# Row sums of a 16384 x 1024 matrix: one of nine loads is summed by one instruction over twelve rows in place of eight paired sums

## The chip, the core and the metric

The kernel runs on one core of a Trainium2 chip. The metric is the device time of one execution in microseconds (us), the median of several runs. The core has VectorE (DVE in the profile), ScalarE (ACT), GpSimd (POOL), TensorE (PE, not used here) and SyncE (SP), each with an instruction queue of its own, and 16 DMA engines that move data between the device memory and the core's SBUF. The only order among the queues is what semaphores enforce. A DMA is issued on a queue (here SP's and, for two stores, ACT's) and lands later; instructions that need its data wait for the landing.

## What is computed

The input has 32 x 512 rows of 1024 float32 values. Every row is summed.

```python
def setup_inputs():
    batch, seq, dim = 32, 512, 1024
    return {"x": np.random.randn(batch, seq, dim).astype(np.float32)}

def reference(x):
    return np.sum(x, axis=-1).astype(np.float32)
```

The input is 67.1 MB, the output 64 KB.

## The kernel before

The 16384 rows are spread over the 128 partitions, 128 rows to a partition, in three blocks: a head of 7 rows per partition (`HEAD`), seven loads of 15 rows each (`BIG`, `LOADS`), and a last block of 16 rows (`LAST`). "A row" below always means one row on each of the 128 partitions, that is 128 x 1024 values. One partition's rows of a block lie side by side in memory, and a load brings n rows to each partition in one DMA. All sums go to one tile, `sums`, with a column for each of the 128 rows (`[P, J]`).

The input tiles `t` come from a pool with three buffers (`bufs=3`, L140), taken in turn: the head has the first, the seven loads the second, third, first, second, third, first and second, and the last block the third. The loads are issued on SP's queue in the order of the program. A load into a buffer waits until the tile that had it before has been read; so the loads of the last block wait for the reduction of the fifth big load.

`rows()` (L182) does one load and sums its rows. It takes the number of rows that ScalarE sums (`n_act`) and whether VectorE sums in pairs. The rest of the rows are VectorE's:

- without `pairs`, one `tensor_reduce` (L148, TENSOR_REDUCE in the profile) reads all of VectorE's rows and writes a sum for each;
- with `pairs`, each row is a `tensor_tensor_reduce` of its own (`halves`, L162; CUSTOM_DVE_ANT_0 in the profile). It adds the second half of the row to the first, writes the 512 results in place, and accumulates their total. Reading the accumulator is a second short instruction (DVE_READ_ACCUMULATOR2_ANT).
- ScalarE's rows are an activation with function Copy each (`act`, L175, ACTIVATE), with a running total that is read out by ACTIVATION_READ_ACCUMULATOR. The copied values go to a PSUM tile, `unread`, that nobody reads (four buffers).

Head and first six big loads use `tensor_reduce` alone, with no ScalarE rows (`rows(t, 0, x_h, 0, 0)` and the `if` in the loop over `g`, L203 to L207). The seventh big load (`g == 6`, L209) gives 7 rows to ScalarE and 8 to VectorE in pairs.

The last block comes in pieces, each a DMA of its own: 7 rows (3 of them ScalarE's), 6 rows (2), 2 rows (1), and the last row in two parts of 536 and 488 values (L224, L225). The last row is summed by two `halves` one after the other: the first leaves its total in the column ahead of the second part, and the second then adds that column with the rest (L228, L229; L222 zeroes the column behind). Three stores write the result: the head's sums early (L200, on ACT's queue), the sums of the seven big loads (L226, `early`, on ACT's queue behind ScalarE's last row, held until the two-row piece has landed), and the last 16 sums (L230, on SP's queue), which end the program.

The order of work on each engine is the order of the program (`manual_schedule`). Three small functions rearrange instructions when the program is finished (first load at the entry, order of the waits of one instruction, a wait at the end); the change doesn't touch them.

Of the kernel before, what the change touches and what calls it, by code (L numbers as in the profile page):

```python
# [101 lines left out]
def kernel(  # L102
# [12 lines left out]
    rows = batch * seq  # L115
    J = rows // P
    HEAD, BIG, LOADS = 7, 15, 7
# [21 lines left out]
    with (  # L139
        tc.tile_pool(name="in", bufs=3) as inpool,  # L140
        tc.tile_pool(name="unread", bufs=4, space=bass.MemoryType.PSUM) as upool,
        tc.tile_pool(name="stage", bufs=1) as stpool,
        tc.manual_schedule(),
    ):
        sums = stpool.tile([P, J], fp32)

        def vec(dst, src):
            return nc.vector.tensor_reduce(  # L148
                out=dst, in_=src, axis=mybir.AxisListType.X, op=mybir.AluOpType.add
            )  # L150

        def hold(inst, until, reason):
            tc.add_manual_dep(
                inst.ins,
                until.ins.name,
                mybir.DependencyInfo(mybir.DependencyClass.Sync, mybir.DependencyReason.DATA),
                reason=reason,
            )

        def halves(dst, src):  # L160
            n = src.shape[-1] // 2
            return nc.vector.tensor_tensor_reduce(  # L162
                out=src[:, :n],
                in0=src[:, :n],
                in1=src[:, n:],
                scale=1.0,
                scalar=0.0,
                op0=mybir.AluOpType.add,
                op1=mybir.AluOpType.add,
                accum_out=dst,  # L170
            )

        def act(dst, src, n):
            unread = upool.tile([P, dim], fp32)
            nc.scalar.activation(  # L175
                out=unread[:, :n],
                in_=src,
                func=mybir.ActivationFunctionType.Copy,
                accum_out=dst,
            )  # L180

        def rows(t, a, src, j, n_act, pairs=False):  # L182
            n = src.shape[1]
            nv = n - n_act
            part = t[:, a * dim : (a + n) * dim].rearrange("p (n d) -> p n d", d=dim)
            load = nc.sync.dma_start(out=part, in_=src)  # L186
            if pairs:
                for q in range(nv):
                    done = halves(sums[:, j + q : j + q + 1], part[:, q, :])
            else:  # L190
                done = vec(sums[:, j : j + nv], part[:, :nv, :])
            for q in range(nv, n):
                act(sums[:, j + q : j + q + 1], part[:, q, :], dim)
            return load, done


        size = LAST * dim + 4
        t = inpool.tile([P, size], fp32)
        rows(t, 0, x_h, 0, 0)
        nc.scalar.dma_start(out=out_h, in_=sums[:, :HEAD])  # L200


        for g in range(LOADS):  # L203
            t = inpool.tile([P, size], fp32)
            src = x_m[:, g * BIG : (g + 1) * BIG, :]
            if g < LOADS - 1:
                rows(t, 0, src, HEAD + g * BIG, 0)  # L207
            else:
                rows(t, 0, src, HEAD + g * BIG, 7, pairs=True)  # L209


        j = HEAD + RUN
        t = inpool.tile([P, size], fp32)
        rows(t, 0, x_l[:, :7, :], j, 3, pairs=True)
        rows(t, 7, x_l[:, 7:13, :], j + 7, 2, pairs=True)
        two, _ = rows(t, 13, x_l[:, 13:15, :], j + 13, 1, pairs=True)


        c, width = pieces
        a = LAST - 1  # L220
        whole = t[:, a * dim + c : LAST * dim + 2]
        nc.vector.memset(whole[:, width + 1 :], 0.0)  # L222
        part = t[:, a * dim : a * dim + c]
        nc.sync.dma_start(out=part, in_=x_l[:, a, :c])  # L224
        nc.sync.dma_start(out=whole[:, 1 : width + 1], in_=x_l[:, a, c:])  # L225
        early = nc.scalar.dma_start(out=out_m, in_=sums[:, HEAD : HEAD + RUN])  # L226
        hold(early, two, "its packets come behind those of the loads")
        halves(whole[:, :1], part)  # L228
        halves(sums[:, J - 1 : J], whole)  # L229
        nc.sync.dma_start(out=out_l, in_=sums[:, j:])  # L230
# [30 lines left out]
```

## Time and profile before

| what | value |
|---|---|
| median of 3 runs | 162.27 us (162.22 to 162.77) |
| the profiled execution, whole | 162.26 us |
| its span in the profile | 160.1 us |
| VectorE busy | 116.1 us (73%) |
| ScalarE busy | 15.2 us (10%) |
| bytes read, mean rate over the span | 67.11 MB, 420 GB/s |

The span is the time from the first to the last instruction of the profiled execution; 2.2 us of its own time lie outside it. The profile names an instruction by line, engine, operation, what it writes and what it reads (`sums<-t`), with shapes as partitions x elements. "Idle before" is the time in which the engine had nothing to do ahead of an instruction, and the name behind the arrow is what ended it. A busy share is an average over stages that may have different limits, so the stage around the change has to be read for itself.

### The profile page before, as it was taken

The numbers are of one execution on the slowest core, as the hardware profiler recorded it, in microseconds if no ns is written. First come the engines' busy times: TensorE is split into PE (matmuls) and PEld (weight loads), VectorE is DVE, ScalarE is ACT, GpSimd is POOL, SyncE is SP. The second block draws the span as 40 slices with busy tenths as digits, with TensorE's granted clock in tenths as the row PEclk, the third lists the DMA queues.
The fourth block names the chain that finished last, engine by engine and source line by source line (L and its number), as shares of the span: only waits on it lengthen the run. The fifth ranks groups of instructions, "written<-read, shape, count | busy, mean of one in ns | idle before, by whom it ended". The sixth has DMA issues, their size and how long they took to land.

```text
span 160.1 us, 148 instructions
## 1 busy us (share of the span) xinstructions
DVE 116.1 (73%) x46; ACT 15.2 (10%) x27; POOL 0.2 (0%) x4
## 2 busy tenths in 40 slices
DVE  0029600699959998699959999599959999573345
ACT  0000210000000000000000000000000000496443
POOL 0000000000000000000000000000000000000000
DMA  8899997999699979998899969996999799899992
GB/s 301 387 475 491 491 415 323 492 492 445 292 491 491 461 307 461 491 491 368 368 491 491 445 292 491 491 461 276 491 491 461 307 461 491 344 451 410 418 390 98
DMA packets 2304, 67.18 MB, mean 420 GB/s; under 512 B 640, under 2 KB 768, under 8 KB 896
## 3 DMA queue, kind: packets, MB, share of 16 engines
q1 hardware_dynamic: 2016, 67.12, 97.6%
q10 hardware_dynamic: 288, 0.06, 0.2%
HBM read 67.11 MB, written 0.07 MB: 420 GB/s over the span
## 4 chain that ended last, share of the span: by engine, by line
DMA 76%; DVE 20%; SPq 1%; issue 0%; DVEq 0%
DMA t<-in_x_dram 76%; DVE sums L148 20%; SPq L186 1%; SPq L224 0%; DVE t L162 0%; DVEq L256 0%
## 5 line engine op out<-in xcount | busy, mean ns | idle before, releaser
L148 DVE TENSOR_REDUCE sums<-t 128x15 f32<-128x15360 f32 (+1 forms) x7 | 104.5, 14934 | 31.6 <-DMA t<-in_x_dram 31.6
L175 ACT ACTIVATE unread<-t 128x1024 f32<-128x1024 f32 x13 | 13.2, 1013 | 123.3 <-DMA t<-in_x_dram 123.3
L162 DVE CUSTOM_DVE_ANT_0 t<-t 128x512 f32<-128x512 f32 (+2 forms) x19 | 11.5, 661 | 10.6 <-DMA t<-in_x_dram 10.4
L175 ACT ACT_TABLE_LOAD x1 | 1.3, 1283 | 19.2 <-DVE sums L148 19.2
L175 ACT ACTIVATION_READ_ACCUMULATOR unread<-t 128x1 f32 x13 | 2.4, 186 | 0.0
L162 DVE DVE_READ_ACCUMULATOR2_ANT sums<- 128x1 f32 x18 | 1.5, 83 | 0.0
L245 POOL MEMSET const-bfloat16-1.0<- 128x1 bf16 x1 | 0.1, 102 | 0.0
L245 POOL MEMSET const-uint8-127<- 128x1 uint8 x1 | 0.1, 102 | 0.0
L245 POOL MEMSET const-float32-1.0<- 128x1 f32 x1 | 0.1, 99 | 0.0
L245 POOL MEMSET const-float32-0.0<- 128x1 f32 x1 | 0.1, 98 | 0.2 <-issue 0.2
L162 DVE DVE_READ_ACCUMULATOR2_ANT t<- 128x1 f32 x1 | 0.1, 83 | 0.0
L222 DVE MEMSET t<- 128x1 f32 x1 | 0.1, 59 | 0.0
## 6 DMA issues: line engine op xcount, KB each, us to landing
t<-in_x_dram SPq DMA_DIRECT2D x7, 7680.0 KB, 38.2
t<-in_x_dram SPq DMA_DIRECT2D x2, 3584.0 KB, 19.9
t<-in_x_dram SPq DMA_DIRECT2D x1, 3072.0 KB, 35.7
t<-in_x_dram SPq DMA_DIRECT2D x1, 1024.0 KB, 37.7
t<-in_x_dram SPq DMA_DIRECT2D x1, 268.0 KB, 37.9
t<-in_x_dram SPq DMA_DIRECT2D x1, 244.0 KB, 38.0
out_dram<-sums ACTq DMA_DIRECT2D x1, 52.5 KB, 1.7
out_dram<-sums ACTq DMA_DIRECT2D x1, 3.5 KB, 21.8
```

The lines of the kernel that those rows point to most:

```text
L148: return nc.vector.tensor_reduce(out=dst, in_=src, axis=mybir.AxisListType.X, op=mybir.AluOpType.add)
L162: return nc.vector.tensor_tensor_reduce(out=src[:, :n], in0=src[:, :n], in1=src[:, n:], scale=1.0, scalar=0.0, op0=mybir.AluOpType.add, op ...
L175: nc.scalar.activation(out=unread[:, :n], in_=src, func=mybir.ActivationFunctionType.Copy, accum_out=dst,)
L186: load = nc.sync.dma_start(out=part, in_=src)
L222: nc.vector.memset(whole[:, width + 1 :], 0.0)
L245: nc = _bacc.Bacc("TRN2", target_bir_lowering=False, num_devices=1)
```

## The change

In the seventh big load, ScalarE gets 3 rows in place of 7, and VectorE's 12 rows are one `tensor_reduce` in place of 8 paired sums.

```diff
             if g < LOADS - 1:
                 rows(t, 0, src, HEAD + g * BIG, 0)
             else:
-                rows(t, 0, src, HEAD + g * BIG, 7, pairs=True)
+                rows(t, 0, src, HEAD + g * BIG, 3)
```

The load itself, its place in SP's queue, and all that follows in the program are the same text.

## The prediction

> **What bounds the kernel now.** I read the chain of work that ended last first, because it says which resource an edit must touch to move the end; then the same chain in order of time, for its last part; then the groups kept apart by shape, for prices; then the timeline from 120 us on, where the changed load is summed.
>
> The page's chain:
>
> ```profile
> DMA t<-in_x_dram 76%; DVE sums L148 20%; SPq L186 1%; SPq L224 0%; DVE t L162 0%; DVEq L256 0%
> ```
>
> The chain in order of time (start us, us, what), its last pieces:
>
> ```profile
> 101.86 16.16 DVE sums L148
> 118.02 0.02 issue
> 118.04 0.33 SPq L186
> ...
> 119.42 0.43 SPq L224
> 119.85 0.04 issue
> 119.89 37.98 DMA t<-in_x_dram
> 157.87 0.02 issue
> 157.90 0.42 DVE t L162
> ```
>
> The 20% of VectorE in the chain are two reductions, and the later one is the fifth big load's (101.86 to 118.02): it frees the buffer for the last block, whose loads are then issued at once. From 119.89 to 157.87 the chain is nothing but those loads on their way. So the end is set by when the last bytes land, and every load has been issued before the changed rows are touched at 138.15. Only three things in the change could move the end: VectorE being late for the last row, ScalarE being late, or the transfers themselves becoming faster or slower.
>
> Prices, by shape (busy us, mean ns, idle before):
>
> ```profile
> L148 DVE TENSOR_REDUCE sums<-t 128x15 f32<-128x15360 f32 x6 | 96.9, 16153 | 20.5 <-DMA t<-in_x_dram 20.5
> L148 DVE TENSOR_REDUCE sums<-t 128x7 f32<-128x7168 f32 x1 | 7.6, 7620 | 11.1 <-DMA t<-in_x_dram 11.1
> ```
>
> And the timeline of the stage (start us, us, engine, instruction):
>
> ```profile
> 120.00 16.15 DVE L148 TENSOR_REDUCE sums<-t 128x15 f32<-128x15360 f32 x1 [1.99 <-DMA t<-in_x_dram]
> 138.15 1.03 ACT L175 ACTIVATE unread<-t 128x1024 f32<-128x1024 f32 x1 [117.67 <-DMA t<-in_x_dram]
> 138.16 0.69 DVE L162 CUSTOM_DVE_ANT_0 t<-t 128x512 f32<-128x512 f32 x1 [2.00 <-DMA t<-in_x_dram]
> ...
> 143.06 0.08 DVE L162 DVE_READ_ACCUMULATOR2_ANT sums<- 128x1 f32 x1
> ...
> 146.82 0.69 DVE L162 CUSTOM_DVE_ANT_0 t<-t 128x512 f32<-128x512 f32 x1 [3.68 <-DMA t<-in_x_dram]
> ...
> 149.28 0.08 DVE L162 DVE_READ_ACCUMULATOR2_ANT sums<- 128x1 f32 x1
> ...
> 154.13 0.69 DVE L162 CUSTOM_DVE_ANT_0 t<-t 128x512 f32<-128x512 f32 x1 [4.77 <-DMA t<-in_x_dram]
> ...
> 156.69 0.34 ACTq L226 DMA_DIRECT2D out_dram<-sums  x1
> 157.25 0.08 DVE L162 DVE_READ_ACCUMULATOR2_ANT sums<- 128x1 f32 x1
> 157.28 0.06 DVE L222 MEMSET t<- 128x1 f32 x1
> 157.30 0.44 DVE L162 CUSTOM_DVE_ANT_0 t<-t 128x268 f32<-128x268 f32 x1
> ```
>
> The reader is to see VectorE finish the seventh load at 143.14 (143.06 + 0.08), wait 3.68 us for the 7-row piece, finish that at 149.36 and wait 4.77 us for the 6-row piece. These two waits are the cover under which the change's extra work must fit.
>
> **VectorE's part.** Removed: eight pairs, 138.16 to 143.14, 4.98 us. Added: one reduction of 12 rows. The trace has 7 rows (7.620 us) and 15 rows (16.153 us); the slope is (16.153 - 7.620) / 8 = 1.0666 us a row, so 12 rows take 7.620 + 5 x 1.0666 = 12.95 us. The difference is 7.97 us more VectorE work. It begins when the load lands, as the pairs did, and ends at 138.16 + 12.95 = 151.11. The 7-row piece has by then been there since 146.82, so its four pairs follow directly: 149.36 - 146.82 = 2.54 us, to 153.65. The 6-row piece lands at 154.13. So 7.97 us go into 3.68 + 4.77 = 8.45 us of waiting, and 0.48 us are left: from 154.13 on VectorE runs as before. Price on the path: 0.
>
> If that cover were gone, VectorE would be late at 154.13 by some D. Two more small covers follow: the fifth pair of the last block could start at 156.58 and started with its landing at 156.63 (0.05 us), and the very last sum could start about 157.81, estimated from its predecessor's read at 157.66 plus its 0.08 and a hand-over of the same size, and started at 157.90 (about 0.09 us). So the end moves by D - 0.14, and by over 0.5% (0.81 us, about what a measurement of this kernel can tell from no change) only when VectorE comes 0.48 + 0.14 + 0.81 = 1.43 us later than worked out.
>
> Here the Trainium skill speaks against the change. Its page "VectorE: DVE Perf Modes", section "Rules for kernel authors", says of `tensor_reduce` on a hot path that it is the slowest VectorE operation and to restructure. The rows agree on the ratio (1.067 us a row against 4.98 / 8 = 0.62 us for a pair). With VectorE on the path, the sum would be 7.97 us more, 170.2 us; by the rows of waiting it is 0 and 162.3 us. I go by the rows, since the path is not hot for VectorE here.
>
> **What no row shows.** First, a pair straight behind a reduction: before, 2.00 us of waiting always stood between the last reduction (over at 136.15) and the first pair. The bounds are -0.08 us (pairs start 0.61 us apart though each takes 0.69) and 2.00 us (all that the wait could have hidden). The nearest row is the pair behind the MEMSET, which starts at 157.30, 0.02 us after the MEMSET's start and before its end, with a change of operation in between. I take 0. Second, a reduction while ScalarE also reads: all six long ones ran alone. The bounds are 0 and 2.3%, by which ScalarE's own first row beside a pair (1.03 us) is longer than later ones (1.005): 0.30 us on 12.95. Pairs took 0.69 us throughout beside ScalarE, so I take 0. Both at their upper ends would be 2.30 us.
>
> **ScalarE's part.** Four rows fewer, 1.04 us each from start to start (138.15, 139.21, 140.25). Its three rows end at about 141.4 in place of 145.54, and its next row waits for the landing at 146.82 either way. Cost and gain 0. The store of the big loads' sums (L226) needs all of them: the last is now ready at 151.11, not 145.54, but the store stands behind ScalarE's last row and was issued at 156.69, 5.6 us later. Cost 0 until the reduction ends 5.6 us late. Nothing is queued behind that store on ACT.
>
> **DMA and buffers.** No transfer is added, removed or moved. The second buffer, which holds the seventh load, is not taken again, so releasing it at 151.11 instead of 145.54 delays nobody. SP has issued everything by 120.4 us and then waits for the last sums. The transfers could still feel what the engines do to SBUF. Big loads landed 18.14 us apart (101.86 to 120.00, 120.00 to 138.15), with a reduction beside them nearly all the time; by their rate a 7-row piece takes 18.14 x 7/15 = 8.47 us. The one beside the eight pairs took 146.82 - 138.15 = 8.67 us, 0.20 us more. If pairs or ScalarE's rows are the cause, that much may come back; if reading by two engines at once is, it may grow with the stretch. The bounds are -0.20 us and, for 12.95 us in place of 4.98, 0.20 x 12.95 / 4.98 - 0.20 = +0.32 us. I take 0, as what caused the 0.20 isn't shown.
>
> **The sum** against the profiled execution: span 160.1 + 0 + 0 + 0, and its own time 162.26 us, stays. That execution lies 0.01 us from the median of 162.27, so the forecast is 162.25 us, rounded; its own range is 162.05 to 162.6 by the transfer bounds.
>
> **Rivals.**
>
> *VectorE comes late (slower).* The place is the hand-over from the 12-row reduction to the first pair of the 7-row piece. It costs something between 0 and 2.00 us that the wait before it hid. From 0.62 us on it moves the end, and from 1.43 us on by over 0.5%. At the full 2.00 us, the pairs end at 155.65, D = 1.52, and the end moves by 1.38 us: 163.65 us. For it: the margin is thin, 0.48 us of 8.45, and no row shows this pair of instructions. Against it: the MEMSET's row, and the straight-line price of a reduction, which six rows within 0.002 us of each other support.
>
> *The transfers gain.* The 0.20 us of the 7-row piece come back, and all later pieces land earlier by as much: 162.05 us. VectorE, ready at 153.65, is still ahead of a landing at 153.93. For it: the slow piece is the one beside the eight pairs. Against it: the 6-row piece, beside four pairs, took 7.31 us where the big loads' rate gives 7.26, so pairs alone don't explain it.
>
> *The transfers lose.* Reduction and ScalarE together slow them by up to 0.32 us: 162.6 us, inside 0.5%. Against it: six reductions beside transfers at the full 18.14.
>
> That the edit does less than it says has no footing: the loop's last turn takes the changed branch and no other.
>
> **Chances.** Forecast 0.54, transfers gain 0.14, transfers lose 0.12, VectorE late by enough to show 0.16, and 0.04 for a gain over 0.5% that no row speaks for. So faster 0.04, same 0.80, slower 0.16. The range runs from 161.9, just below the transfers' gain, to 163.1, 0.5% above the time before; the late VectorE at 163.65 and the unexplained gain are what it leaves out, 0.20 together.
>
> **What would show it.** Right: one L148 instruction 128x12 of 12.95 us from about 138.16; the first pair of the 7-row piece at 151.1 with no idle time before it; VectorE idle under 1 us ahead of the 6-row piece and still released by DMA; the last pieces of the chain as before. Wrong: a reduction over 13.4 us, a gap of over half a microsecond behind it, or the chain ending in VectorE rather than in DMA. Landings of the 7-row piece nearer than 8.67 us to the seventh load's would speak for the transfers' gain, and farther ones for their loss.

## The result, and the profile after

| | before | changed |
|---|---|---|
| median of 17 runs each | 162.34 us (162.22 to 162.82) | 161.93 us (161.69 to 162.24) |
| profiled execution, whole | 162.26 us | 161.99 us |
| its span | 160.08 us | 160.20 us |
| whole minus span | 2.18 us | 1.79 us |

The ratio is 0.9971, with a 95% interval of 0.9964 to 0.9979: 0.29% faster, small but clear of the scatter. The last two rows are the surprise: the profiled span has become longer by 0.12 us while the whole time has become shorter by 0.27. Over the 17 runs of the changed kernel the span's median is 160.1 us; over the runs of the kernel before that came with the experiments it is 160.1 to 160.2. Nothing that can be told from scatter was won inside the span.

The first lines of the page of the changed kernel, and its chain:

```profile
span 160.2 us, 123 instructions
...
DMA t<-in_x_dram 77%; DVE sums L148 20%; SPq L186 1%; SPq L224 0%; DVE t L162 0%; DVEq L256 0%
```

Its chain in order of time, the last pieces:

```profile
120.21 37.79 DMA t<-in_x_dram
158.00 0.02 issue
158.03 0.42 DVE t L162
```

Its timeline of the changed stage:

```profile
138.45 12.96 DVE L148 TENSOR_REDUCE sums<-t 128x12 f32<-128x12288 f32 x1 [1.99 <-DMA t<-in_x_dram]
...
146.95 1.03 ACT L175 ACTIVATE unread<-t 128x1024 f32<-128x1024 f32 x1 [5.27 <-DMA t<-in_x_dram]
...
151.32 0.68 DVE L162 CUSTOM_DVE_ANT_0 t<-t 128x512 f32<-128x512 f32 x1
...
154.27 0.69 DVE L162 CUSTOM_DVE_ANT_0 t<-t 128x512 f32<-128x512 f32 x1 [0.42 <-DMA t<-in_x_dram]
...
156.82 0.34 ACTq L226 DMA_DIRECT2D out_dram<-sums  x1
```

The reader is to see that the stage does what was worked out. The 12-row reduction takes 12.96 us; the first pair starts behind it at 151.32 with no idle time; of the 8.45 us in which VectorE waited before, 0.42 are left, ended by the landing of the 6-row piece; the chain is the last loads on their way, as before. The page counts 123 instructions, where the kernel before had 148. Of these, VectorE has 31 where it had 46, and this turned out to be the number that matters.

### The profile page after: what moved, and what is told of

The parts are those of the page before. It is cut to its first block, busy times and chain, and to the rows that moved or that the text cites. A ratio compares the mean times of both kernels' runs of the same rounds, so it can differ in the third digit from the quotient of the medians.

```text
span 160.2 us, 123 instructions
## 1 busy us (share of the span) xinstructions
DVE 124.0 (77%) x31; ACT 11.1 (7%) x19; POOL 0.2 (0%) x4
## 4 chain that ended last, share of the span: by engine, by line
DMA 77%; DVE 20%; SPq 1%; issue 0%; DVEq 0%
DMA t<-in_x_dram 77%; DVE sums L148 20%; SPq L186 1%; SPq L224 0%; DVE t L162 0%; DVEq L256 0%
## 5 line engine op out<-in xcount | busy, mean ns | idle before, releaser
L148 DVE TENSOR_REDUCE sums<-t 128x15 f32<-128x15360 f32 (+2 forms) x8 | 117.5, 14687 | 33.9 <-DMA t<-in_x_dram 33.9
L175 ACT ACTIVATE unread<-t 128x1024 f32<-128x1024 f32 x9 | 9.1, 1016 | 127.3 <-DMA t<-in_x_dram 127.3
L162 DVE CUSTOM_DVE_ANT_0 t<-t 128x512 f32<-128x512 f32 (+2 forms) x11 | 6.5, 641 | 0.6 <-DMA t<-in_x_dram 0.6
L175 ACT ACTIVATION_READ_ACCUMULATOR unread<-t 128x1 f32 x9 | 1.7, 187 | 0.0
L162 DVE DVE_READ_ACCUMULATOR2_ANT sums<- 128x1 f32 x10 | 0.8, 84 | 0.0
```

The costliest lines, as they stand in the source:

```text
L148: return nc.vector.tensor_reduce(out=dst, in_=src, axis=mybir.AxisListType.X, op=mybir.AluOpType.add)
L162: return nc.vector.tensor_tensor_reduce(out=src[:, :n], in0=src[:, :n], in1=src[:, n:], scale=1.0, scalar=0.0, op0=mybir.AluOpType.add, op ...
L175: nc.scalar.activation(out=unread[:, :n], in_=src, func=mybir.ActivationFunctionType.Copy, accum_out=dst,)
```

## The experiments

Two theories stood at the start. **Theory T** (transfers, a rival of the prediction): the 7-row piece lands 8.50 us behind the seventh load (138.45 to 146.95) in place of 8.67, so the pairs or ScalarE's rows had slowed it. **Theory I** (instructions): the time outside the span, whole minus span, depends on the program's instructions. It is a good measure, since each run has both numbers: in the 26 runs of the kernel before that came with the first four experiments, the whole time went from 162.04 to 162.81 us, but whole minus span stayed between 2.13 and 2.23.

Each edit below is against the changed kernel, if nothing else is said. "Outside" is the mean of whole minus span over a run's executions, with spans given to 0.1 us. "VectorE instructions" counts all that the record of the profiled execution has on VectorE's queue, waits and barriers included: 55 before and 39 after (the page counts only the work among them, 46 and 31). ScalarE's are 39 before and 30 after.

### One part of the change at a time, and instructions alone

First run: the seventh load by one reduction, over 8 rows, and 7 rows on ScalarE as in the kernel before.

```diff
-                rows(t, 0, src, HEAD + g * BIG, 3)
+                rows(t, 0, src, HEAD + g * BIG, 7)
```

> Seventh load: one reduction of 8 rows, ScalarE keeps 7 rows. Against before, only the eight pairs are gone (15 VectorE instructions fewer), ScalarE's part is as before. Theory I (instructions: the time outside the span, 2.18 us before and 1.79 us after, follows the number of instructions of the program): outside about 1.95 if all instructions count alike (15 of 25 gone), 1.79 if only VectorE's count; whole time 162.34 - 0.23 = 162.1 or 161.95. Theory T (transfers: the 7-row piece lands 8.67 us behind the seventh load before and 8.50 after, and the pairs are what slows it): piece at 8.50, outside 2.18, whole time about 162.15. If ScalarE's rows slow the piece: 8.67. The reduction should take 8.69 us and end about 0.03 us behind the landing of the piece, which costs nothing.

Second run: 3 rows on ScalarE as in the changed kernel, and VectorE's 12 rows in pairs.

```diff
-                rows(t, 0, src, HEAD + g * BIG, 3)
+                rows(t, 0, src, HEAD + g * BIG, 3, pairs=True)
```

> Seventh load: 12 rows in pairs (24 VectorE instructions), 3 rows on ScalarE (8 fewer than before). The program has as many instructions as before. Theory I with all alike: outside 2.18, whole time 162.34 (same as before); with VectorE's alone: above 2.18, about 2.4, whole time 162.5. Theory T with pairs as the cause: the 7-row piece lands 8.67 us or more behind the seventh load (pairs last 7.4 us in place of 5.0: up to 8.77), whole time 162.34 to 162.45; with ScalarE's rows as the cause: 8.50 to 8.55 and about 162.15.

Third run: the changed kernel with idle instructions on VectorE, in its first wait.

```diff
+        idle = stpool.tile([P, 16], fp32)
+        for q in range(16):
+            nc.vector.memset(idle[:, q : q + 1], 0.0)
         rows(t, 0, x_h, 0, 0)
```

> The changed kernel with 16 one-column MEMSETs on VectorE ahead of the first reduction, where VectorE waits 11 us. No work on the path changes. Theory I: outside goes back by 16/25 of 0.39 us to about 2.04 (all alike) or fully to 2.18 (VectorE's alone); whole time 162.15 to 162.35. Theory T: nothing changes, 161.93, with the piece at 8.50.

Fourth run: the changed kernel with idle instructions on ScalarE.

```diff
+        idle = stpool.tile([P, 16], fp32)
+        nc.vector.memset(idle[:, :8], 0.0)
+        for q in range(4):
+            act(idle[:, 8 + q : 9 + q], idle[:, :8], 8)
         rows(t, 0, x_h, 0, 0)
```

> The changed kernel with four 8-column activations, each with its accumulator read (8 ScalarE instructions, as many as the change removed there), and one MEMSET on VectorE, all in the first 11 us. Theory I, all alike: outside 1.79 + 9/25 of 0.39 = 1.93, whole time 162.07; if ScalarE's instructions alone count: 2.18 and 162.34; if VectorE's alone: 1.79 to 1.81 and 161.95. Theory T: 161.93.

| run | VectorE instr. | median us | ratio to before | outside us |
|---|---|---|---|---|
| reduction of 8, ScalarE 7 | 39 | 161.83 | 0.9969 [0.9956, 0.9981] | 1.79 |
| 12 pairs, ScalarE 3 | 63 | 162.16 | 0.9985 [0.9976, 0.9994] | 1.98 |
| changed + 16 MEMSETs | 55 | 162.34 | 1.0004 [0.9995, 1.0012] | 2.18 |
| changed + 4 activations | 40 | 161.89 | 0.9975 [0.9965, 0.9984] | 1.79 |

Sixteen MEMSETs that do nothing for the result, in a stretch where VectorE waits anyway, take the whole gain back. Eight extra instructions on ScalarE do nothing. The twelve pairs were expected above 2.18 us by the reading that more VectorE instructions cost more; they gave 1.98, with more instructions. So it isn't a price per instruction.

Theory T has no footing in these runs: the 7-row piece came 8.52 us behind the seventh load beside twelve pairs, and 8.59 beside the 8-row reduction. Runs below settle it.

### The shape: how outside time goes with VectorE's instructions

The same edit with other numbers of MEMSETs (4, 8, 12, 14, 20, 24, 32, 40) in the changed kernel.

> The changed kernel with 4 one-column MEMSETs ahead of the first reduction, as 16 of them in the run that gave 2.18 us outside the span (39 VectorE instructions in the profile without them, 55 with 16). Theory I-slope (each VectorE instruction adds 0.39/16 = 0.024 us outside the span): outside 1.89, whole time 162.0. Theory I-step (the outside time jumps where VectorE's program passes some length): outside 1.79 or 2.18 and nothing between.

> The same with 8 MEMSETs (47 VectorE instructions). Theory I-slope: outside 1.99. Theory I-step: 1.79 or 2.18.

> The same with 12 MEMSETs (51 VectorE instructions). Theory I-slope: outside 2.08. Theory I-step: 1.79 or 2.18, and 2.18 if 8 already gave it.

> The same with 24 MEMSETs, which makes 63 VectorE instructions, as many as the kernel with 12 pairs and 3 ScalarE rows, whose outside time was 1.97. If the number of VectorE instructions sets the outside time whatever their kind: 1.97 here too, below the 2.18 of 16 MEMSETs, so no slope and no single step. If the kind matters (MEMSETs of line 201 against pairs in the middle of the program): the slope gives 1.79 + 24 x 0.024 = 2.37, a single step 2.18.

> The changed kernel with 14 MEMSETs, 53 VectorE instructions. The outside time was 1.79 at 51 and 2.18 at 55. Theory boundary (a fetch of VectorE's program comes into the end once the program passes a boundary): 1.79 or 2.18, a jump between two neighbours. Theory of a gradual rise: about 1.98.

> The same with 20 MEMSETs, 59 VectorE instructions, between 55 (2.18) and 63 (1.96). Theory boundary, with the fetch triggered ever earlier as more of the program lies behind the boundary: between 2.18 and 1.96, about 2.07. If 63 is a plateau of its own: 2.18 or 1.96.

> The same with 40 MEMSETs, 79 VectorE instructions. Theory boundary, with the fetch ever earlier and at last hidden under the span: 1.79, and the instruction packet no longer behind the span's end. If the program beyond 63 costs as much as at 63: 1.96. If every instruction beyond adds time: above 2.2.

> The changed kernel with 32 MEMSETs, 71 VectorE instructions. From 55 to 63 the outside time fell by 0.027 us an instruction; at 71 that gives 1.75, so the floor of 1.79 or just above it, with the instruction packet at the end of the span or earlier. Theory moved cost: if the packet comes while loads still run, span 160.4 and whole time 162.2; if it comes behind the last load (157.6) and before the end, span 160.1 and 161.9. Theory hidden cost: 161.9 either way.

| VectorE instr. | kernel | outside us | span median us | whole median us | ratio to before |
|---|---|---|---|---|---|
| 39 | changed | 1.78 | 160.1 | 161.93 | 0.9971 [0.9964, 0.9979] |
| 43 | + 4 | 1.80 | 160.1 | 161.91 | 0.9978 [0.9966, 0.9990] |
| 47 | + 8 | 1.79 | 160.2 | 161.99 | 0.9985 [0.9973, 0.9996] |
| 51 | + 12 | 1.78 | 160.3 | 162.05 | 0.9975 [0.9962, 0.9987] |
| 53 | + 14 | 1.78 | 160.1 | 161.86 | 0.9968 [0.9955, 0.9981] |
| 55 | + 16 | 2.18 | 160.2 | 162.34 | 1.0004 [0.9995, 1.0012] |
| 59 | + 20 | 2.08 | 160.1 | 162.18 | 1.0001 [0.9989, 1.0014] |
| 63 | + 24 | 1.95 | 160.25 | 162.18 | 0.9994 [0.9983, 1.0005] |
| 71 | + 32 | 1.78 | 160.4 | 162.19 | 0.9994 [0.9985, 1.0003] |
| 79 | + 40 | 1.79 | 160.45 | 162.23 | 0.9992 [0.9981, 1.0004] |

A flat floor up to 53, a jump of 0.4 us within the next two instructions, then a fall of about 0.03 us an instruction to the floor again. The trace shows what falls. Each row below is a stretch of half a microsecond, with its length, the busy time of VectorE, ScalarE and GpSimd, the clock, the DMA engines' share and GB/s; behind it, in a fence of its own, the line of the DMA view for what lies after the span. With 20 MEMSETs:

```profile
161.40:161.90 0.50, 0.00 (x0) 0.00 (x0) 0.00 (x0) 1.00 0.00 0
161.90:162.40 0.50, 0.00 (x0) 0.00 (x0) 0.00 (x0) 1.00 0.05 16
```

```profile
q14 instruction: 1, 0.01, 1.0%
```

With 24:

```profile
161.40:161.90 0.50, 0.00 (x0) 0.00 (x0) 0.00 (x0) 1.00 0.05 16
161.90:162.40 0.50, 0.00 (x0) 0.00 (x0) 0.00 (x0) 1.00 0.00 0
```

One packet of instructions, 8192 bytes, starts 1.87 us behind the span's end with 59 VectorE instructions and 1.14 us behind it with 63. With 40 MEMSETs (79) it has moved into the span, to 143.49 us, between the packets of the loads. The DMA view from 143 to 144 us:

```profile
q1 hardware_dynamic: 15, 0.43, 103.9%
q14 instruction: 1, 0.01, 2.0%
```

With 71 it stands at 152.18 us. With 53 or fewer, no packet of instructions stands near the end or later than the first microsecond of the span. With 55, where the outside time is longest, none is in the record either; by the others it would start later still, and whether it comes too late to be recorded stays open.

So from some length of VectorE's program on, a packet of instructions is recorded late, and the more of the program there is, the earlier it comes. Whether it is one packet more in all can't be counted, as the records hold between 4 and 7 packets of this size ahead of the span, whatever the kernel. The record names no engine for it; it is taken for VectorE's because its time follows VectorE's count.

With the packet inside the span the gain does not come back. The span's medians with 71 and 79 are 160.4 us, 0.3 us above the changed kernel's; the outside time is back at its floor, and the whole time, at 162.2 us, is not. That the packet takes this time from the loads is shown only in part. It takes 0.31 us (79) and 0.33 us (71), and in the record one packet of the loads starts as it ends and takes 1.72 us where others of its size take 1.06 (with 71, 1.57 where others take 0.91). So it holds up one stream of the loads; whether that is the stream that the end waits for is another matter. The last loads in the chain with 71:

```profile
120.61 37.78 DMA t<-in_x_dram
```

With 79:

```profile
120.14 37.97 DMA t<-in_x_dram
```

The changed kernel has 37.79 and the kernel before 37.98, both with no such packet. In the profiled execution with 71 the packet therefore cost the end nothing; its span, 160.60 us, is long because the first load landed at 11.81 us, where the changed kernel's landed at 11.43. The idle MEMSETs themselves are a rival for the longer spans: 24 of them, with the packet behind the span, gave 160.25 us. What lengthens the spans at 71 and 79 stays open.

### The same in the kernel before, with the seventh load untouched

Fewer VectorE instructions (48), with the eight pairs and ScalarE's seven rows kept:

```diff
-        rows(t, 0, x_l[:, :7, :], j, 3, pairs=True)
+        rows(t, 0, x_l[:, :7, :], j, 3)
```

> The kernel before, with its eight pairs in the seventh load and ScalarE's 7 rows kept. Only the 4 VectorE rows of the 7-row piece are one reduction, which takes 4.42 us (7.620 - 3 x 1.0666) and ends at 151.24, before the landing at 154.13. VectorE has 48 instructions in place of 55. Theory length (the number of VectorE's instructions sets the time outside the span: 1.79 from 39 to 51, 2.18 at 55, 1.96 at 63): outside 1.79, whole time 161.95. Theory seventh load (what the change does to the seventh load's rows is the cause): nothing changes, 162.3.

More (63 and 79), as the MEMSETs above with 8 and 24 in the kernel before:

> The kernel before with 8 one-column MEMSETs ahead of the first reduction, 63 VectorE instructions. Theory length: outside 1.96, so more instructions and a shorter time, 162.1, and an instruction packet of 8 KB a good microsecond behind the span's end, as in the kernel of 12 pairs. Theory seventh load, and any theory by which instructions cost time each: 162.3 or more.

> The kernel before with 24 one-column MEMSETs, 79 VectorE instructions. With 79 in the changed kernel the outside time was back at 1.79 and an instruction packet of 0.31 us stood at 143.5, inside the span, on one of the 16 DMA engines that carry the loads; its eight spans were 160.2 to 160.5, median 160.45, where the changed kernel's median is 160.1. Theory moved cost (the packet takes its 0.3 us from the loads when it comes before the end): outside 1.79, span 160.4, whole time 162.2. Theory hidden cost (it is free inside the span): outside 1.79, span 160.15, whole time 161.95.

| run | VectorE instr. | median us | ratio to before | outside us | span median us |
|---|---|---|---|---|---|
| piece of 7 rows by one reduction | 48 | 161.95 | 0.9977 [0.9969, 0.9986] | 1.78 | 160.2 |
| before + 8 MEMSETs | 63 | 162.16 | 0.9990 [0.9981, 0.9999] | 1.96 | 160.2 |
| before + 24 MEMSETs | 79 | 162.22 | 0.9994 [0.9986, 1.0003] | 1.79 | 160.4 |

The first gives the change's gain with nothing of the change in it. The second adds instructions, and its time outside the span falls from 2.18 to 1.96 us, with a packet behind the span as in the changed kernel with 24 MEMSETs. The DMA view of that kernel from 160 to 165 us:

```profile
q14 instruction: 1, 0.01, 0.4%
```

The third has the floor outside, and its span is 0.3 us longer than the 160.1 us of the kernel before run beside it; here the packet stands at 144.69 us, inside the span. Each came out within 0.03 us of the outside time expected.

### ScalarE's program

```diff
+        idle = stpool.tile([P, 20], fp32)
+        nc.vector.memset(idle[:, :8], 0.0)
+        for q in range(12):
+            act(idle[:, 8 + q : 9 + q], idle[:, :8], 8)
         rows(t, 0, x_h, 0, 0)
```

> The changed kernel with 12 short activations and their accumulator reads on ScalarE, about 56 ScalarE instructions and 40 VectorE ones. If the boundary holds for each engine's own program at the same length: 2.18 here as with 55 VectorE instructions. If VectorE's alone, or another length on ScalarE: 1.79.

Outside 1.94 us, whole 162.06 us, ratio 0.9985 [0.9973, 0.9996], with 56 ScalarE instructions and 40 on VectorE. So a longer ScalarE program can bring a cost outside the span too; neither expectation named this value. Where its boundary lies wasn't measured, and no packet of instructions is recorded behind this span.

### Is VectorE's margin as thin as the profile says?

The seventh load wholly on VectorE, 15 rows in one reduction:

```diff
-                rows(t, 0, src, HEAD + g * BIG, 3)
+                rows(t, 0, src, HEAD + g * BIG, 0)
```

> Seventh load wholly one reduction of 15 rows. VectorE is now late: in the changed kernel's profile the reduction began at 138.45 and the pairs behind it ended 0.42 us before the 6-row piece. Three rows more take 3.20 us, so VectorE is 2.78 us late for that piece, and the end moves by 2.78 - 0.14 = 2.64 us: span 162.75, outside 1.79, whole time 164.5. If VectorE were no closer to the path than its share says, or the later pieces had more room: 161.9 to 163.

162.7 us of span in the profiled execution and 164.58 us whole (two runs), ratio 1.0139 [1.0120, 1.0157]: 0.1 us from the expectation. Its timeline:

```profile
138.36 16.15 DVE L148 TENSOR_REDUCE sums<-t 128x15 f32<-128x15360 f32 x1 [2.00 <-DMA t<-in_x_dram]
154.43 0.68 DVE L162 CUSTOM_DVE_ANT_0 t<-t 128x512 f32<-128x512 f32 x1
...
156.88 0.69 DVE L162 CUSTOM_DVE_ANT_0 t<-t 128x512 f32<-128x512 f32 x1
...
160.53 0.42 DVE L162 CUSTOM_DVE_ANT_0 t<-t 128x245 f32<-128x245 f32 x1
```

No wait for DMA stands in brackets behind the reduction: VectorE is the path from there on, and the last sum starts 22.17 us behind the seventh load's landing where the changed kernel has 19.58. Three rows more than the change turn a gain of 0.4 us into a loss of 2.2.

### A version with fewest VectorE instructions

The 8-row reduction with ScalarE's 7 rows, and the 7-row piece by one reduction as well: 32 VectorE instructions.

```diff
-                rows(t, 0, src, HEAD + g * BIG, 3)
+                rows(t, 0, src, HEAD + g * BIG, 7)
...
-        rows(t, 0, x_l[:, :7, :], j, 3, pairs=True)
+        rows(t, 0, x_l[:, :7, :], j, 3)
```

> Reductions both in the seventh load (8 rows, ScalarE 7) and in the 7-row piece (4 rows): 32 VectorE instructions, the fewest. Both fit under the landings (8.69 us to 146.9, then 4.42 to 151.3, before 154.1). Theory length, with a flat stretch below 51: outside 1.79, 161.9, no better than the changed kernel. If a lower step exists below 39: less outside than 1.79 and a version faster than both.

161.88 us, ratio 0.9975 [0.9964, 0.9986], outside 1.79 us: the floor, and no better than the changed kernel. No version here beats it beyond the intervals.

## Why the prediction was right about the span and wrong about the time

**The step that failed** is the last one, the sum "against the profiled execution": "its own time 162.26 us, stays". It carried the 2.18 us outside the span over as a constant. They became 1.78 us, and that difference of 0.40 is nearly all of the gain of 0.41. The step goes back to the sentence "Only three things in the change could move the end": VectorE, ScalarE and the transfers are three things inside the span. The prediction priced the removed pairs by the time that they were busy and never asked what a shorter program does. The page had VectorE's count, 46 instructions, and nothing in the profile before said that it was worth anything: no late packet of instructions is in its record.

All the signs that the prediction named for being right came true inside the span, and the time moved all the same. That 161.93 us lies within its range, by 0.03 us, is luck: the lower end, 161.9, had been set by the transfers. And 0.5% was too coarse for what a measurement of this kernel can tell: 0.29% came out clear of the scatter.

**VectorE's part** held. 12.95 us for the reduction (12.96 measured), end of the pairs at 153.65 from a landing at 138.16 (15.49 us; measured 138.45 to 153.85, 15.40), 0.48 us of cover left (0.42). The unpriced hand-over from a reduction to a pair cost -0.09 us, at the lower of its two bounds (-0.08), and the reduction beside ScalarE's rows kept its price to 0.01 us. The late-VectorE rival fell with that, but its place was right: in the 15-row run the last sum came 2.59 us later, where the covers of 0.42 (measured) and 0.14 us gave 2.64.

**ScalarE's part, the store, the queues and buffers** cost nothing, as worked out: ScalarE waited 5.27 us for the 7-row piece in place of 1.28, and the store left at 156.82.

**The rival "transfers gain"** comes nearest in its number, 162.05 us, and for a wrong reason. The piece did land 8.50 us behind the seventh load. But in the changed kernel with 8 idle MEMSETs, with the same reduction and the same three ScalarE rows, it took 8.71:

```profile
138.42 1.03 ACT L175 ACTIVATE unread<-t 128x1024 f32<-128x1024 f32 x1 [117.67 <-DMA t<-in_x_dram]
...
147.13 1.03 ACT L175 ACTIVATE unread<-t 128x1024 f32<-128x1024 f32 x1 [5.49 <-DMA t<-in_x_dram]
```

And with the eight pairs and ScalarE's seven rows kept, in the kernel before with 8 MEMSETs, it took 8.51:

```profile
138.46 0.69 DVE L162 CUSTOM_DVE_ANT_0 t<-t 128x512 f32<-128x512 f32 x1 [2.00 <-DMA t<-in_x_dram]
...
146.97 0.69 DVE L162 CUSTOM_DVE_ANT_0 t<-t 128x512 f32<-128x512 f32 x1 [3.53 <-DMA t<-in_x_dram]
```

This gap differs from execution to execution by 0.2 us, and a single profile before can't tell such scatter from an effect. So neither the pairs nor ScalarE's rows are what made it 8.67, and the span's medians, equal within 0.1 us, leave no gain of 0.2 us to the transfers.

**What stays open.** The runs show that the time outside the span goes with the length of VectorE's program, whatever its instructions are, and that a packet of instructions comes earlier as the program grows. They don't show what is paid for outside the span, nor on which side of it, nor why the boundary lies between 53 and 55 recorded instructions for this kernel. It isn't a plain wait for the packet to land: with 59 instructions the packet takes 0.44 us and ends 2.31 us behind the span, but that execution's whole time is only 2.07 us longer than its span. The Trainium skill, page "Runtime: NRT & Kernel Launch", section "Instruction fetch mechanics", says that an engine's instructions are brought in by DMA while it runs and that crossing a block's boundary is mostly hidden. The runs agree with the first part: a packet of instructions came at 152.18 us with 71 instructions, while the program ran. Whether the jump between 53 and 55 is such a boundary no run shows; it cost 0.4 us at its worst, outside the span.

## What to carry to other kernels

Subtract the span from the whole time before and after, in every run: when an edit that is fully covered in the span still moves the time, the difference shows it at once, with a scatter of about 0.03 us where the whole time has some 0.15. In this kernel, whose end is set by transfers, the number of VectorE's instructions had a price of its own, which jumped between 53 and 55 and then fell; whether another kernel has such a jump, and where, has to be measured, and idle instructions ahead of the first wait are a cheap probe for it. Before moving work onto an engine with waits, add up the waits that the stage has, as here 8.45 us for 7.97, and expect the end to move by whatever doesn't fit.

## What the runs showed of the hardware that was not expected

- The time outside the span is 1.78 to 1.80 us for 32 to 53 recorded VectorE instructions, 2.18 at 55, 2.08 at 59, 1.95 to 1.98 at 63, and 1.78 to 1.79 at 71 and 79.
- A packet of instructions, 8192 bytes and some 0.3 to 0.5 us, stands behind the span at 59 and 63 and inside it at 71 and 79, where the span's median is 0.3 us longer.
- One packet of the loads that starts as the instruction packet ends takes 1.57 to 1.72 us, where others of its size take 0.91 to 1.06 (71 and 79).
- With 56 recorded ScalarE instructions and 40 on VectorE, the time outside is 1.94 us, where 40 and 40 gave 1.79.
- A pair that follows a reduction directly starts 0.09 us before the reduction's recorded end (0.08 in the 15-row run).
